# A hybrid streaming-encoder layer on one core: the decay chain begun directly behind the token factor

## The chip, the cores and the metric

The kernel runs on one core of a Trainium2 chip. The metric is the device time of one execution in microseconds (us). Five engines work beside each other and meet only through semaphores: TensorE (PE in the profile, its weight loads PEld), VectorE (DVE), ScalarE (ACT), GpSimd (POOL) and SyncE (SP), whose queue issues most of the transfers.

## The reference

One layer of a trunk over 512 tokens with 1024 channels, all in float32. What matters here is the first part:

```python
xn = rmsnorm(h, mix_norm_w)
proj = xn @ w_in                      # gates, gMLP, z, xBC, dt
...
xbc = jax.nn.silu(causal_dwconv(xbc, conv_w, conv_b))      # 4 taps; xs, B, C
dt = jax.nn.softplus(dt_raw + dt_bias)
A = -jnp.exp(a_log)
...
a_cum = jnp.cumsum(dt * A, axis=2)
decay = jnp.exp(where(causal, a_cum[l] - a_cum[s], -inf))
y_diag = einsum(C·B, decay, x * dt);  states and y_off use exp(a_cum)
```

Behind it come a gated gMLP branch, the projections of both branches, a ConvGLU feed-forward part and a last RMSNorm. None of that is touched.

## The kernel before

Channels lie on the 128 partitions and the 512 tokens in the free dimension. Every projection goes through `cols`: a unit of 256 output channels fills two PSUM accumulators of 128x512, from two halves (`kb`) of four input tiles each. To keep float32 precision each operand is split in a high and a low part (ACT copies the high part, DVE subtracts), and each product takes three matmuls, so a unit of K=1024 is 48 matmuls of 128x512. The weights come through `weights`, with four buffers each for the raw, high and low parts.

The normalisation is postponed. The first two units (`B0` and `C0`, a half of B and of C) multiply the input times the norm's weight (`xw`), not yet divided by the token's root mean square. Meanwhile the token factor `rb` is made (`x_norm`: sums by matmuls, a power on POOL, a broadcast by matmuls, a copy on ACT). Then `unnorm` scales the finished accumulators by `rb`, and `x_split` makes the normalised, split input `xn` for all later units.

The order of the work from there on is: `C0`, then the units `x0`, `x2`, `x4`, `x6` (xs, channels 0 to 1023), `B2`, `C2`, then `x8` to `x14`. Each unit is followed by `conv`, on both accumulators: ACT starts the sum from PSUM (L341), DVE adds three shifted taps from PSUM (L343), ACT applies Silu (L345). An accumulator comes free at the third tap. There are four such PSUM buffers in rotation (`PM`), so a unit waits until the convolution of the unit two before has read its accumulators: `x8p` needs those of `B2p`, `x10p` those of `C2p`.

The decay chain `dt_chain` is a generator in pieces: dt_raw scaled by `rb` (`dtraw`), its transposes (`dttok`), the softplus as a row of some twenty small DVE instructions (`dttmp`, 128x128), the cumulative sums as two matmuls (`acp`), copies and exponentials of these (`ac_k`, `decb`, `dd_k`), transposes (`ach`), and two copies (`achs`, `eahs`) that go out to DRAM (`acum_d`, `ea_d`). Each `ssm_step` loads them back, broadcast over the partitions (`s0bc`, `s0ea` for the first pair of heads), and the decay matrices are made from these.

`defer` and `tick` say in which step of the matmul loop a piece is recorded: each `kb` of `cols` is one tick. The table `CHAIN` holds the ticks for the pieces of the chain. That is the order of recording. In it, PE is written out by hand for the first two units only (`manual_schedule`); from there a scheduler with a model of the engines sets the order on PE, ACT, DVE, POOL and the SP queue. Engines take their instructions strictly in that order.

Of the kernel before, what the change touches and what calls it, by code (L numbers as in the profile page):

```python
# [33 lines left out]
def kernel(  # L34
# [15 lines left out]
    def T(name, dt=F32):  # L50
        return tp.tile([P, S], dt, tag="t", name=name)
# [4 lines left out]
    def PA(name):  # L56
        return pp.tile([P, S], F32, tag="aux", name=name, bufs=4)
# [31 lines left out]
    def cols(w, u, xs, name):  # L89

        K = len(xs)
        ps = [PM(f"{name}p{i}") for i in range(2)]
        nb = K // 4
        for kb in range(nb):
            hi, lo = weights(w[u, kb], [P, 4, 2 * P], f"{name}w{kb}")

            def mm(i, k, part):
                xh, xl = xs[4 * kb + k]
                c = slice(i * P, (i + 1) * P)
                if part == 0:  # L100
                    pe.matmul(ps[i], lhsT=hi[:, k, c], rhs=xh, start=(kb == 0 and k == 0), stop=False)  # L101
                    pe.matmul(ps[i], lhsT=hi[:, k, c], rhs=xl, start=False, stop=False)  # L102
                else:
                    pe.matmul(ps[i], lhsT=lo[:, k, c], rhs=xh, start=False, stop=(kb == nb - 1 and k == 3))  # L104

            if name in BYK:
                order = [(i, k, part) for k in range(4) for part in range(2) for i in range(2)]
            elif kb < nb - 1:
                order = [(i, k, part) for part in range(2) for k in range(4) for i in range(2)]
            else:  # L110
                order = [(i, k, part) for i in range(2) for part in range(2) for k in range(4)]
            for o in order:
                mm(*o)
            tick()
        return ps
# [4 lines left out]
    def defer(fn, n=1):  # L120
        later.append([n, fn])
# [86 lines left out]
    def rstd(ssq, n, name):  # L208

        m = ssq.shape[-1]  # L210
        v = sm.tile([P, m], F32, tag="rsv", name=name + "v")
        dve.tensor_scalar(out=v, in0=ssq, scalar1=1.0 / n, scalar2=EPS, op0=ALU.mult, op1=ALU.add)  # L212
        r = sm.tile([P, m], F32, tag="rsr", name=name + "r")
        pool.tensor_tensor(out=r, in0=v, in1=mhalf[:, :m], op=ALU.pow)  # L214
        return r

    def token_sums(sq, name):

        ps = PA(name)
        n = sq.shape[-1] // P  # L220
        for c in range(n):
            pe.matmul(ps[:, 2 * c:2 * c + 2], lhsT=sq[:, c * P:(c + 1) * P], rhs=ones[:, 0:2], start=True, stop=True)
        return ps[:, 0:2 * n].rearrange("p (c t) -> p c t", t=2)[:, :, 0]

    def bcast_tokens(r, name):

        ps = PA(name)
        n = r.shape[-1]
        for c in range(n):
            pe.matmul(ps[:, c * P:(c + 1) * P], lhsT=r[:, c:c + 1].to_broadcast([P, P]), rhs=ident,  # L230
                      start=True, stop=True)
        return ps[:, 0:n * P]
# [16 lines left out]
    def x_split():  # L249
        ns = []  # L250
        for k in range(KD):
            n = T(f"xn{k}")
            dve.scalar_tensor_tensor(out=n, in0=xT[k], scalar=x0[:, S + k:S + k + 1], in1=rb, op0=ALU.mult, op1=ALU.mult)
            ns.append(n)
            if k:
                xn.append(split(ns[k - 1], f"xn{k - 1}", pool if k in XPOOL else None))
        xn.append(split(ns[-1], f"xn{KD - 1}"))
# [3 lines left out]
    def dt_product():  # L261
        for k in range(KD):
            for i in range(2):
                pe.matmul(dtp[:2 * HEADS], lhsT=wd2[:, k, :], rhs=xw[k][i], start=(k == 0 and i == 0),
                          stop=(k == KD - 1 and i == 1))
# [8 lines left out]
    def flat(t):  # L274
        return t.rearrange("p c h -> p (c h)")

    def dt_chain():

        H = HEADS
        H2 = 2 * H  # L280
        raw = T("dtraw")
        dve.tensor_tensor(out=raw[:H2], in0=dtp[:H2], in1=rb[:H2], op=ALU.mult)
        ps = PA("dttok")
        for c in range(NT):
            pe.transpose(out=ps[:, c * H2:(c + 1) * H2], in_=raw[:H2, c * P:(c + 1) * P], identity=ident[:H2, :H2])
        ps = ps[:, 0:NT * H2].rearrange("p (c h) -> p c h", h=H2)
        tmp = T("dttmp").rearrange("p (i c h) -> p i c h", i=4, h=H)
        xv, e, q, y = (tmp[:, i] for i in range(4))
        dve.tensor_tensor(out=xv, in0=ps[:, :, 0:H], in1=dtb.unsqueeze(1).to_broadcast([P, NT, H]), op=ALU.add)
        dve.tensor_tensor(out=xv, in0=ps[:, :, H:H2], in1=xv, op=ALU.add)  # L290
        act.activation(out=e, in_=xv, func=AF.Abs)
        act.activation(out=e, in_=e, func=AF.Exp, scale=-1.0)
        act.activation(out=alog, in_=alog, func=AF.Exp)
        yield

        with tc.high_priority():
            dve.tensor_scalar(out=q, in0=e, scalar1=2.0, scalar2=None, op0=ALU.add)
            dve.reciprocal(out=q, in_=q)
            dve.tensor_tensor(out=y, in0=e, in1=q, op=ALU.mult)
            dve.tensor_tensor(out=q, in0=y, in1=y, op=ALU.mult)  # L300
            dve.tensor_scalar(out=e, in0=q, scalar1=1.0 / 15, scalar2=None, op0=ALU.mult)
            for d in (13, 11, 9, 7, 5, 3):
                dve.scalar_tensor_tensor(out=e, in0=e, scalar=1.0 / d, in1=q, op0=ALU.add, op1=ALU.mult)
            dve.scalar_tensor_tensor(out=e, in0=e, scalar=1.0, in1=y, op0=ALU.add, op1=ALU.mult)
            dve.tensor_scalar(out=xv, in0=xv, scalar1=0.0, scalar2=None, op0=ALU.max)
            dve.scalar_tensor_tensor(out=dt_k, in0=e, scalar=2.0, in1=xv, op0=ALU.mult, op1=ALU.add)
            dve.scalar_tensor_tensor(out=y, in0=dt_k, scalar=-1.0, in1=alog.unsqueeze(1).to_broadcast([P, NT, H]),
                                     op0=ALU.mult, op1=ALU.mult)

        yield  # L310
        ps = PA("acp")
        pe.matmul(ps[:, 0:P], lhsT=tri, rhs=flat(y), start=True, stop=True)
        pe.matmul(ps[:, P:2 * P], lhsT=ones, rhs=flat(y), start=True, stop=True)
        yield
        act.copy(out=flat(ac_k), in_=ps[:, 0:P])
        act.activation(out=flat(decb), in_=ps[:, P:2 * P], func=AF.Exp)
        dve.tensor_tensor(out=flat(dd_k), in0=ps[:, P:2 * P], in1=flat(ac_k), op=ALU.subtract)
        act.activation(out=dd_k, in_=dd_k, func=AF.Exp)
        dve.tensor_tensor(out=dd_k, in0=dd_k, in1=dt_k, op=ALU.mult)
        pt = PA("ach")  # L320
        for c in range(NT):
            pe.transpose(out=pt[:H, c * P:(c + 1) * P], in_=ac_k[:, c, :], identity=ident)
        yield
        ach = T("achs")
        act.copy(out=ach[:H], in_=pt[:H])
        sync.dma_start(out=acum_d, in_=ach[:H])
        eah = T("eahs")
        act.activation(out=eah[:H], in_=pt[:H], func=AF.Exp)
        sync.dma_start(out=ea_d, in_=eah[:H])
        yield  # L330


    def unnorm(ps, name):
        u = T(name)
        dve.tensor_tensor(out=u, in0=ps, in1=rb, op=ALU.mult)
        return u
# [147 lines left out]
    with tc.manual_schedule(engines={mybir.EngineType.PE}):  # L484
        ps = cols(w_in, U_B, xw, "B0")

        def x_norm():
            r1 = rstd(token_sums(xacc, "xss"), D, "xr")
            dt_product()
            act.copy(out=rb, in_=bcast_tokens(r1, "rbp"))  # L490
            us2.extend(unnorm(ps[q], f"B0u{q}") for q in range(2))
            x_split()

        us2 = []
        defer(x_norm)
        psC = cols(w_in, U_C, xw, "C0")
    us = [unnorm(psC[q], f"C0u{q}") for q in range(2)]
    chain = dt_chain()
    next(chain)
    for n in CHAIN:  # L500
        defer(lambda: next(chain), n)
    for i in (0, 2, 4, 6):
        if i >= 4:
            q = i // 2 - 2
# [263 lines left out]

T_BUFS = 73
XPOOL = ()  # L770
CHAIN = (1, 5, 9, 10)
BYK = ("B0", "x0")
WARM = 10

# [51 lines left out]
```

## Time and profile before

| | |
|---|---|
| time, median of 3 runs | 1027.45 us (1027.16 to 1027.64) |
| the profiled execution | 1028.71 us |
| its span, first to last instruction | 1027.0 us |
| mean granted TensorE clock | 0.995 |
| PE busy | 1014.9 us (99%) |
| DVE busy | 616.5 us (60%) |
| ACT busy | 450.2 us (44%) |
| POOL busy | 41.9 us (4%) |

Busy time is the union of an engine's instructions. In rows of the timeline the columns are the start in us, the length in us, the engine, the line of the kernel, the operation, output and inputs, and how many instructions the row merges; in brackets stands the idle time before it, and what ended that. The matmuls and most others are pipelined: the step from one start to the next is shorter than the length of one.

### The profile page before, as it was taken

To read this page: it belongs to the slowest core of one execution; us is meant where nothing else is said; L and a number is where in the kernel's file an instruction comes from. 1 tells how busy PE (TensorE), PEld (TensorE's weight loads), DVE (VectorE), ACT (ScalarE), POOL (GpSimd) and SP (SyncE) were. 2 spreads that over 40 slices of the span, in tenths; PEclk is the share of its full clock that TensorE was granted. 3 is DMA by queue.
4 is the path that set the end of the run, shared out by engine and by line. 5 is a ranking of instruction groups with operands and counts; after the bars stand their busy time and mean duration, and the time that the engine had idled before them with its cause. 6 is when DMAs were issued, how large, how long until landed. Compare 5 with 4: busy or idle time off the path is not lost.

```text
span 1027.0 us, 12488 instructions
## 1 busy us (share of the span) xinstructions
PE 1014.9 (99%) x4856; PEld 840.3 (82%) x4856; DVE 616.5 (60%) x1006; ACT 450.2 (44%) x613; POOL 41.9 (4%) x72
## 2 busy tenths in 40 slices
PE   9999899999999999999999999999999999999997
PEld 7888788888888888888888888888888888888885
DVE  7795987878796554354123445477668677742224
ACT  7465675665564333363322223354444444331122
POOL 1000000220000200000000000000000000000000
PEclk9999899999999999999999999999999999999999
DMA  7323445423333233323322332232223233323302
GB/s 273 110 83 111 151 144 165 143 94 121 114 125 113 72 97 110 113 85 100 102 97 88 103 102 86 100 114 92 91 93 96 91 101 103 97 89 103 99 25 83
DMA packets 36157, 109.85 MB, mean 107 GB/s; under 512 B 4657, under 2 KB 4929, under 8 KB 36097
## 3 DMA queue, kind: packets, MB, share of 16 engines
q1 hardware_dynamic: 35056, 106.68, 31.8%
q0 software_dynamic: 608, 1.58, 0.5%
q8 instruction: 38, 0.62, 0.3%
q10 hardware_dynamic: 432, 0.79, 0.2%
q14 instruction: 23, 0.18, 0.1%
HBM read 106.80 MB, written 2.24 MB: 106 GB/s over the span
## 4 chain that ended last, share of the span: by engine, by line
PE 98%; DMA 1%; issue 0%; DVE 0%; ACT 0%; POOLq 0%; POOL 0%; SPq 0%
PE dn L726 11%; PE vp L526 1%; PE vp L528 1%; PE vp L527 1%; PE pb6p L101 1%; PE pb4p L101 1%; PE pb2p L101 1%; PE pb0p L101 1%; PE pb6p L104 1%; PE pb4p L104 1%; PE pb2p L104 1%; PE pb0p L104 1%; PE pb6p L102 1%; PE pb4p L102 1%; PE pb2p L102 1%; PE pb0p L102 1%
## 5 line engine op out<-in xcount | busy, mean ns | idle before, releaser
L397 ACT ACT_TABLE_LOAD x15 | 19.2, 1283 | 3.1 <-DMA s15bc<-acum_d 1.6
L764 POOL TENSOR_TENSOR fsr<-fs,mhalf 128x1 f32<-128x1 f32 x4 | 2.2, 548 | 354.9 <-DVE fs L762 354.9
L657 ACT ACTIVATE hh<-hT,pcol 128x512 fp32r<-128x512 f32 x8 | 5.8, 722 | 15.0 <-DVE hT L655 15.0
L756 ACT ACTIVATE fj<-htok 128x512 f32<-128x512 f32 x8 | 5.1, 632 | 16.6 <-DVE htok L754 16.6
L345 ACT ACT_TABLE_LOAD x8 | 10.3, 1283 | 3.9 <-DVE B2c L343 3.0
L214 POOL TENSOR_TENSOR hrr<-hrv,mhalf 128x4 f32<-128x4 f32 x1 | 1.0, 1042 | 248.0 <-DVE hrv L212 248.0
L631 DVE TENSOR_TENSOR m<-m,sa 128x512 f32<-128x512 f32 x8 | 5.5, 688 | 8.6 <-ACT sa L630 8.6
L754 DVE TENSOR_TENSOR htok<-dn,htok 128x512 f32<-128x512 f32 x8 | 5.5, 692 | 8.0 <-PE dn L726 7.9
L612 DVE TENSOR_TENSOR yq<-yq,zs 128x512 f32<-128x512 f32 x12 | 8.2, 685 | 1.5 <-ACT zs L611 1.4
L562 PEld LDWEIGHTS sp<-wsT,v 128*128 128x128 f32 x64 | 7.8, 191 | 0.3
L659 DVE SCALAR_TENSOR_TENSOR hl<-hT,pcol,hh 128x512 fp32r<-128x512 f32 x8 | 6.0, 747 | 3.2 <-ACT hh L657 3.2
L562 PE MATMUL sp<-wsT,v 128*128 128x128 f32 x64 | 7.8, 275 | 0.0
L538 DVE BATCH_NORM_STATS2 bst<-v 128x6 f32<-128x128 f32 x32 | 7.1, 280 | 0.3
L534 ACT ACTIVATE v<-vp 128x512 f32<-128x512 f32 x8 | 4.8, 594 | 3.6 <-PE vp L528 3.6
L565 DVE SCALAR_TENSOR_TENSOR sv<-sp,pcol,radd 128x512 f32<-128x512 f32 x8 | 6.0, 746 | 0.0
L343 DVE SCALAR_TENSOR_TENSOR B2c<-B2p,pcol,B2c 128x511 f32<-128x511 f32 (+2 forms) x6 | 4.2, 742 | 2.5 <-ACT B2c L341 2.5
L694 ACT COPY htok<-htp 128x512 f32<-128x512 f32 x8 | 4.7, 588 | 2.3 <-PE htp L692 2.3
L143 PE MATMUL warm<-ones 128*128 128x128 f32 x20 | 4.6, 429 | 1.1 <-POOL ones L138 1.1
L568 DVE TENSOR_TENSOR sv<-sv,gu 128x512 f32<-128x512 f32 x8 | 5.5, 688 | 0.3
L645 DVE TENSOR_TENSOR sb<-sb,m 128x512 f32<-128x512 f32 x8 | 5.5, 689 | 0.1
L343 DVE SCALAR_TENSOR_TENSOR x14c<-x14p,pcol,x14c 128x511 f32<-128x511 f32 (+2 forms) x6 | 4.5, 747 | 1.5 <-ACT x14c L341 1.4
L743 DVE SCALAR_TENSOR_TENSOR htok<-htok,fsr,fnw 128x512 f32<-128x512 f32 x7 | 5.0, 745 | 0.7 <-POOL fsr L764 0.7
(4034 smaller groups left out, 3501.2 us busy)
## 6 DMA issues: line engine op xcount, KB each, us to landing
out_dram<-htok SPq DMA_DIRECT2D x7, 256.0 KB, 2.0
xT<-in_xt_dram SPq DMA_DIRECT2D x4, 256.0 KB, 6.8
yrb<-yr_d POOLq DMA_DIRECT2D x4, 256.0 KB, 3.5
first<-in_w_in_dram SPq DMA_DIRECT2D x3, 256.0 KB, 7.0
xT<-in_xt_dram POOLq DMA_DIRECT2D x2, 256.0 KB, 7.0
C0w0r<-in_w_in_dram SPq DMA_DIRECT2D x1, 512.0 KB, 7.4
C0w1r<-in_w_in_dram SPq DMA_DIRECT2D x1, 512.0 KB, 7.3
x0w0r<-in_w_in_dram SPq DMA_DIRECT2D x1, 512.0 KB, 5.3
```

Of the source, the lines that this page charges most:

```text
L101: pe.matmul(ps[i], lhsT=hi[:, k, c], rhs=xh, start=(kb == 0 and k == 0), stop=False)
L102: pe.matmul(ps[i], lhsT=hi[:, k, c], rhs=xl, start=False, stop=False)
L104: pe.matmul(ps[i], lhsT=lo[:, k, c], rhs=xh, start=False, stop=(kb == nb - 1 and k == 3))
L343: dve.scalar_tensor_tensor(out=c[:, j:], in0=u[:, :S - j], scalar=pc(R_CW + 24 * (3 - j) + t), in1=c[:, j:], op0=ALU.mult, op1=ALU.add)
L345: act.activation(out=c, in_=c, func=AF.Silu)
L397: act.activation(out=bc, in_=bc, func=AF.Exp)
L526: pe.matmul(ps[t], lhsT=xh[:, ts], rhs=hi[:, k, :], start=(kb == 0 and k == 0), stop=False)
L527: pe.matmul(ps[t], lhsT=xl[:, ts], rhs=hi[:, k, :], start=False, stop=False)
L528: pe.matmul(ps[t], lhsT=xh[:, ts], rhs=lo[:, k, :], start=False, stop=(kb == 3 and k == 1))
L562: pe.matmul(sp[:, t * P:(t + 1) * P], lhsT=vn[t][b][:, gg:gg + P], rhs=wsT[b][:, gg:gg + P], start=True, stop=True)
L612: dve.tensor_tensor(out=acc, in0=acc, in1=zs, op=ALU.add)
L726: pe.matmul(po[t][b], lhsT=l[:, ts], rhs=r[:, cs], start=(k == 0 and l is xh and r is hi), stop=(k == NFF - 1 and r is lo))
```

## The change

The chain's object is created and its first piece recorded inside `x_norm`, directly behind the copy of the token factor, ahead of the scaling of `B0` and of `x_split`. The first piece is cut in two: the multiplication `dtraw` alone, then a new `yield`, then the rest. `CHAIN` gets five entries instead of four. Since `x_norm` runs at the first tick of `C0`, and before the chain was created behind the second and last tick of `C0`, the ticks compare so: the transposes are recorded at the end of `C0` as before, now ahead of the scaling of `C0`'s accumulators, the softplus at the same tick, the cumulative sums at the same tick, the copies behind them and the transposes `ach` one tick earlier, and the two copies to DRAM one tick earlier.

```diff
         dve.tensor_tensor(out=raw[:H2], in0=dtp[:H2], in1=rb[:H2], op=ALU.mult)
+        yield
         ps = PA("dttok")
...
             act.copy(out=rb, in_=bcast_tokens(r1, "rbp"))
+            chain = dt_chain()
+            next(chain)
+            for n in CHAIN:
+                defer(lambda: next(chain), n)
             us2.extend(unnorm(ps[q], f"B0u{q}") for q in range(2))
             x_split()
...
     us = [unnorm(psC[q], f"C0u{q}") for q in range(2)]
-    chain = dt_chain()
-    next(chain)
-    for n in CHAIN:
-        defer(lambda: next(chain), n)
...
-CHAIN = (1, 5, 9, 10)
+CHAIN = (1, 2, 6, 9, 10)
```

The scheduler turns this into another order on every engine, from the first `xs` unit to the gMLP's first unit (`vp`); behind that the rows stand as before. Lines behind the new `yield` count one higher, so L343 of before is L344.

First place, DVE behind the token factor (`rb`); `xn_...` are normalised input tiles, `xn0l` the low part of the first. Before:

```order
L335 TENSOR_TENSOR B0u_326<-B0p_215,rb 128x512
L335 TENSOR_TENSOR B0u_328<-B0p_216,rb 128x512
L253 SCALAR_TENSOR_TENSOR xn_330<-x0m,rb 128x512
L253 SCALAR_TENSOR_TENSOR xn_332<-xT_104,x0m,rb 128x512
L70 TENSOR_TENSOR xn0l<-xn_330,xn0h 128x512
```

The same place on DVE in the changed kernel:

```order
L282 TENSOR_TENSOR dtraw<-dtp,rb 64x512
L336 TENSOR_TENSOR B0u_328<-B0p_215,rb 128x512
L336 TENSOR_TENSOR B0u_330<-B0p_216,rb 128x512
L253 SCALAR_TENSOR_TENSOR xn_332<-x0m,rb 128x512
L253 SCALAR_TENSOR_TENSOR xn_334<-xT_104,x0m,rb 128x512
L70 TENSOR_TENSOR xn0l<-xn_332,xn0h 128x512
```

The multiplication `dtraw` moved from behind all the splits to their head. On PE its four transposes (`dttok`) moved with it, from the middle of `x2` to directly ahead of the first matmul of `x0`.

Second place, ACT around the copies that go to DRAM (`achs`, `eahs`). Before:

```order
L315 COPY ac_k<-acp 128x128
L316 ACT_TABLE_LOAD
L316 ACTIVATE decb<-acp 128x128
L85 ACTIVATE x10w0h<-x10w0r 128x1024
L318 ACTIVATE dd_k<-dd_k 128x128
L325 COPY achs<-ach 32x512
L328 ACTIVATE eahs<-ach 32x512
L341 ACTIVATE B2c_840<-B2p_762,pcol 128x512
L341 ACTIVATE B2c_846<-B2p_763,pcol 128x512
```

The same stretch on ACT in the changed kernel, first the part from `ac_k` on (L346 is the convolutions' Silu):

```order
L316 COPY ac_k<-acp 128x128
L317 ACT_TABLE_LOAD
L317 ACTIVATE decb<-acp 128x128
L346 ACT_TABLE_LOAD
L346 ACTIVATE B0c_676<-B0c_676 128x512
L85 ACTIVATE C2w1h<-C2w1r 128x1024
L346 ACTIVATE C0c_682<-C0c_682 128x512
L342 ACTIVATE x6c_766<-x6p_689,pcol 128x512
L319 ACT_TABLE_LOAD
L319 ACTIVATE dd_k<-dd_k 128x128
L346 ACT_TABLE_LOAD
L346 ACTIVATE x6c_760<-x6c_760 128x512
```

and, following on ACT directly, the part with the two copies:

```order
L326 COPY achs<-ach 32x512
L329 ACT_TABLE_LOAD
L329 ACTIVATE eahs<-ach 32x512
L85 ACTIVATE x8w0h<-x8w0r 128x1024
L346 ACT_TABLE_LOAD
L346 ACTIVATE x6c_766<-x6c_766 128x512
L342 ACTIVATE B2c_840<-B2p_772,pcol 128x512
L85 ACTIVATE x8w1h<-x8w1r 128x1024
L342 ACTIVATE B2c_846<-B2p_773,pcol 128x512
L346 ACTIVATE B2c_840<-B2c_840 128x512
```

The copies stood behind the cast of `x10`'s first weights (`x10w0h`); now they stand ahead of `x8`'s (`x8w0h`), and between `ac_k` and the start of `B2`'s convolution there are six loads of an activation table where there was one. On PE the cumulative sums (`acp`) moved from the middle of `C2` into the last half of `x6`, and the transposes (`ach`) from the end of `C2` into `B2`, behind its first 15 matmuls.

Third place, DVE at the convolution of `B2` (`B2c_840` and `B2c_846`, three taps each, that free the buffers for `x8p`). Before:

```order
L343 SCALAR_TENSOR_TENSOR B2c_840<-B2p_762,pcol,B2c_840 128x511
L343 SCALAR_TENSOR_TENSOR B2c_846<-B2p_763,pcol,B2c_846 128x511
L343 SCALAR_TENSOR_TENSOR B2c_840<-B2p_762,pcol,B2c_840 128x510
L343 SCALAR_TENSOR_TENSOR B2c_846<-B2p_763,pcol,B2c_846 128x510
L86 TENSOR_TENSOR x10w1l<-x10w1r,x10w1h 128x1024
L395 TENSOR_SCALAR s0bc_852<-s0bc_852,ac_k 128x128 x3
L343 SCALAR_TENSOR_TENSOR B2c_840<-B2p_762,pcol,B2c_840 128x509
```

In the changed kernel DVE has there:

```order
L86 TENSOR_TENSOR x8w0l<-x8w0r,x8w0h 128x1024
L344 SCALAR_TENSOR_TENSOR B2c_840<-B2p_772,pcol,B2c_840 128x511
L344 SCALAR_TENSOR_TENSOR B2c_840<-B2p_772,pcol,B2c_840 128x510
L344 SCALAR_TENSOR_TENSOR B2c_840<-B2p_772,pcol,B2c_840 128x509
L86 TENSOR_TENSOR x8w1l<-x8w1r,x8w1h 128x1024
L344 SCALAR_TENSOR_TENSOR B2c_846<-B2p_773,pcol,B2c_846 128x511
L396 TENSOR_SCALAR s0bc_852<-s0bc_852,ac_k 128x128 x4
L344 SCALAR_TENSOR_TENSOR B2c_846<-B2p_773,pcol,B2c_846 128x510
L396 TENSOR_SCALAR s0bc_854<-s0bc_854,ac_k 128x128 x4
L344 SCALAR_TENSOR_TENSOR B2c_846<-B2p_773,pcol,B2c_846 128x509
```

The first accumulator's three taps are done ahead of the first work on the loaded decay rows (`s0bc`); the second one's last two taps still stand behind it. On the SP queue the writes of `acum_d` and `ea_d` moved ahead of the load of `x12w0r`, and the loads of `s0bc` directly behind that, ahead of `x12w1r` and `x14w0r`.

## The prediction

> **What bounds the kernel now.** I read the page first, then who waits for whom, then stretches, then the timeline of each engine around the one stretch that stands out. The page:
>
> ```profile
> span 1027.0 us, 12488 instructions
> PE 1014.9 (99%) x4856; PEld 840.3 (82%) x4856; DVE 616.5 (60%) x1006; ACT 450.2 (44%) x613; POOL 41.9 (4%) x72
> ```
>
> PE bounds the kernel, and the change adds and removes no matmul. So it can only change PE's waits. All of PE's waits (us in total, times, longest):
>
> ```profile
> PE x8p L101 <- DVE B2c L343: 3.5, 1, 3.5
> PE warm L143 <- POOL ones L138: 1.1, 1, 1.1
> PE B0p L101 <- ACT B0w0hi L201: 0.7, 1, 0.7
> ```
>
> The last two lie ahead of anything the change touches. The first is the target. Stretches around it (busy us of PE, PEld, DVE, ACT, POOL; granted clock; DMA), and its matmuls:
>
> ```profile
> 100.00:105.00 5.00, 2.60 (x20) 2.19 (x18) 3.89 (x8) 2.99 (x5) 0.00 (x0) 1.00 0.50 163
> 105.00:110.00 5.00, 3.93 (x9) 3.14 (x10) 5.00 (x14) 3.94 (x5) 0.00 (x0) 0.53 0.92 251
> 110.00:115.00 5.00, 5.00 (x19) 4.02 (x18) 5.00 (x15) 4.09 (x5) 0.00 (x0) 0.79 0.55 188
> ...
> 102.00 0.60 PE L384 MATMUL s0xt<-ident,x0c 128*128 128x128 f32 x4
> 106.07 0.76 PE L101 MATMUL x8p<-xn0h,x8w0h 128*128 128x512 f32 x1 [3.47 <-DVE B2c L343]
> 106.63 0.63 PE L102 MATMUL x8p<-xn0l,x8w0h 128*128 128x512 f32 x1
> 112.15 0.39 PE L101 MATMUL x8p<-xn5h,x8w1h 128*128 128x512 f32 x1
> 112.38 0.40 PE L102 MATMUL x8p<-xn5l,x8w1h 128*128 128x512 f32 x1
> ```
>
> PE stands still for 3.47 us, and then the clock is down: 14 matmuls fill 106.07 to 112.15, 6.08 us, where at the later step (112.38 - 112.15 = 0.23, 0.227 over longer stretches) they take 3.18. The stall costs 3.47 + 2.90 = 6.37 us. What made it, engine by engine:
>
> ```profile
> 88.60 0.39 PE L104 MATMUL B2p<-xn7h,B2w1l 128*128 128x512 f32 x1
> ...
> 97.86 0.58 ACT L325 COPY achs<-ach 32x512 f32<-32x512 f32 x1 [2.21 <-PE ach L322]
> 98.34 0.58 ACT L328 ACTIVATE eahs<-ach 32x512 f32<-32x512 f32 x1
> 98.83 1.42 ACT L341 ACTIVATE B2c<-B2p,pcol 128x512 f32<-128x512 f32 x2
> ...
> 98.47 2.45 DMA acum_d<-achs
> 100.94 3.63 DMA s0bc<-acum_d
> ...
> 104.59 0.68 DVE L395 TENSOR_SCALAR s0bc<-s0bc,ac_k 128x128 f32<-128x128 f32 x3 [1.11 <-DMA s0bc<-acum_d]
> 105.19 0.74 DVE L343 SCALAR_TENSOR_TENSOR B2c<-B2p,pcol,B2c 128x509 f32<-128x509 f32 x1
> ```
>
> `B2p` is complete at 89, but ACT starts its convolution at 98.83, because that stands behind `achs`, which waited for the chain. The last tap then stands on DVE behind `s0bc`, which waits for the chain's round trip through DRAM. The tap ends at 105.93, and `x8p` starts at 106.07. Both queues were blocked by the chain being late.
>
> **The change, part by part.** *The head of the chain.* Its rows:
>
> ```profile
> 42.32 0.70 PE L102 MATMUL x0p<-xn6l,x0w1h 128*128 128x512 f32 x2
> 49.09 0.46 PE L285 MATMUL dttok<-ident,dtraw 64*128 64x64 f32 x4
> ...
> 41.56 0.68 DVE L70 TENSOR_TENSOR xn6l<-xn,xn6h 128x512 fp32r<-128x512 f32 x1
> 43.96 0.67 DVE L282 TENSOR_TENSOR dtraw<-dtp,rb 64x512 f32<-64x512 f32 x1
> ```
>
> `dtraw` ahead of the splits moves each of them back by 0.60 to 0.67 us. There is no room for that: `xn6l` is done at 42.24 and its matmul starts at 42.32. But the transposes now stand ahead of `x0` and move PE back by 0.4 to 0.6 too, time that they took inside `x2` before. I charge the difference, 0.1 us, with 0 and 0.3 as ends.
>
> *The softplus and the sums.*
>
> ```profile
> 72.05 0.74 DVE L343 SCALAR_TENSOR_TENSOR C0c<-C0u,pcol,C0c 128x511 f32<-128x511 f32 x1
> 87.28 0.29 DVE L307 SCALAR_TENSOR_TENSOR dttmp<-dt_k,alog 128x128 f32<-128x128 f32 x1
> ...
> 76.14 0.39 PE L101 MATMUL x6p<-xn6h,x6w1h 128*128 128x512 f32 x1
> 92.01 0.38 PE L312 MATMUL acp<-dttmp,tri 128*128 128x128 f32 x2
> ```
>
> The chain's last small product, done at 87.6 before, now stands directly ahead of that first tap of the second `C0c`, at 72.05 before. Ahead of it come some seven more small steps (0.2 to 0.3 each, as the 0.29 here) and one tap more, so it ends by 72 to 74. The sums now stand behind the `x6p` matmul of 76.14. They find their input ready and run at 76.4 instead of 92.01; `ach` runs at 81.8 (`B2` starts at 78.3, plus 15 times 0.227). PE gains nothing and loses nothing by the moves themselves.
>
> *ACT, the new narrow place.*
>
> ```profile
> 92.65 0.27 ACT L315 COPY ac_k<-acp 128x128 f32<-128x128 f32 x1 [3.47 <-PE acp L313]
> 92.94 1.28 ACT L316 ACT_TABLE_LOAD   x1
> 94.23 0.28 ACT L316 ACTIVATE decb<-acp 128x128 f32<-128x128 f32 x1
> 94.40 1.05 ACT L85 ACTIVATE x10w0h<-x10w0r 128x1024 fp32r<-128x1024 f32 x1
> ...
> 95.89 1.22 DVE L86 TENSOR_TENSOR x10w0l<-x10w0r,x10w0h 128x1024 fp32r<-128x1024 f32 x1
> 99.62 2.73 DVE L343 SCALAR_TENSOR_TENSOR B2c<-B2p,pcol,B2c 128x511 f32<-128x511 f32 x4 [2.52 <-ACT B2c L341]
> ```
>
> From `ac_k` at 77.0 to `achs` ACT has four loads (5.2), three 128-wide steps (0.9), three Silus (0.6 each, from the 0.58 of `eahs`), one weight cast (1.0) and one convolution start (0.7): 9.6 us, so `achs` ends at 87.2, 11 us earlier than before, though `ach` was ready at 82.3. Then a load and `eahs` to 89.1, `x8w0h` to 90.1, a load and a Silu to 92.0, the start of the first `B2c` to 92.7, `x8w1h` to 93.7, the second start to 94.4.
>
> *SP and the round trip.* `acum_d` is written by 87.2 + 2.45 = 89.7. The load of `x12w0r` ahead of `s0bc` waits for DVE's `x8w0l`, 90.1 + 1.2 = 91.3. So `s0bc` is issued at about 91.8. Issue to landing, from the DMA table:
>
> ```profile
> s0bc<-acum_d SPq DMA_DIRECT2D x2, 256.0 KB, 3.8
> s2bc<-acum_d SPq DMA_DIRECT2D x2, 256.0 KB, 8.0
> ```
>
> I take 5, near the row of the same load, with something for the weight load in front; the ends are 3.8 and 8.0. It lands at 96.8 (95.6 to 99.8). DVE meanwhile does the first `B2c` (three taps of 0.68, to 94.8), `x8w1l` (96.0) and one tap of the second (96.7). Behind the landing come 2 x 4 small steps (0.23 each, from 0.68 for three; 1.8) and two taps (1.4): 100.0, at worst 103.0. PE, with nothing missing, ends `s0xt` at 102.6 and needs the second accumulator two matmuls later, at 103.05. The wait is gone over the whole range.
>
> *What is late next: `x10p`,* on the convolution of `C2`:
>
> ```profile
> 119.87 0.83 PE L406 MATMUL s0st<-s0xdd,btok 128*128 128x128 f32 x6
> 120.53 0.60 PE L384 MATMUL s1xt<-ident,x0c 128*128 128x128 f32 x4
> ```
>
> ACT starts it 6.1 us behind the landing (two loads, two exponentials, a cast, a Silu, the start), and DVE needs 10.4 more for what stands there (six taps 4.1, a split 1.2, two rounds of four small steps 1.8, five products of 0.65, as the 0.68 of `xn6l`): landing + 16.5 = 113.3, at worst 116.3. PE wants it at 102.6 + 48 x 0.227 + 1.2 for the two rows + 0.45 = 115.15. Slack 1.9 us; at worst a wait of 1.2. The loads of `x12w0r` and `x12w1r`, on SP behind the chain now, land by 100 and are wanted behind `x10p`, after 125: no price.
>
> *Sum:* -3.47 - 2.90 + 0.1 + 0.1 for small slips = -6.2 us. The profiled execution took 1028.71, 1.7 outside its span and 1.26 above the median. I take the difference as equal in both: 1027.45 - 6.2 = 1021.2.
>
> **The rivals.**
> *A part only (0.20).* Either a wait of 1 to 3.4 us stays at `x8p` or `x10p`, if my ACT sum is some us short: 1022.5 to 1025. Or the half clock behind the stall belongs to the profiled execution alone, and only 3.5 us is won: 1024.0. Three runs within 0.48 us speak against executions that differ by 2.9, so most of the 0.20 is the first case.
>
> [...] The trace shows the clock falling after 3.47 us of idleness.
>
> *No change (0.10), in one of two ways.* First (0.04), ACT's table loads cost more than their rows. [...] The rows speak against it: from the end of `ac_k` (92.92) to `decb` (94.23) pass 1.31 us, the load and nothing else.
>
> [...]
>
> Second (0.06), DVE sets the pace from `x8` on, and PE only meets it later:
>
> ```profile
> 120.00:160.00 40.00, 40.00 (x218) 33.10 (x217) 34.57 (x71) 28.39 (x36) 2.41 (x6) 1.00 0.44 136
> ```
>
> DVE has 5.4 us to spare in 40 there, but PE would come 6.4 earlier. If the convolutions keep their times, the waits come at `x12p` to `vp` and sum to most of the gain: 1026.5 to 1028. Against it: by the sum above `C2` is done 1.9 us before PE wants it, and from there DVE has its 5.4 us in 40 to stay ahead.
>
> *Slower (0.08).* `s0bc`, now in flight with `x12w0r`, lands late. At a landing of 103 the wait at `x8p` is 3.2 and the clock's price about makes it the old stall; from 106 on, 14 us after issue, it is over 1030. The slowest row has 8.0.
>
> **How the numbers follow.** The likeliest, the whole stall gone, gets 0.62: 1021.2 (1020.5 to 1022). With the part case the range is 1020.4 to 1025.2, some 0.82. Half a spread of the runs shown is 0.24 us; 0.2% is 2.05 us, about what a measurement can tell from no change. Faster: 0.62 + 0.20 = 0.82; same 0.10; slower 0.08.
>
> **What would show it.** No PE wait at `x8p`, a granted clock of 1.00 from 100 to 115, `acp` near 76.4, `achs` near 87, `s0bc` landing by 97, `x8p` starting near 102.6, and a span near 1020.8. I am wrong if ACT reaches `achs` after 91, if `x10p`, `x12p` or `vp` wait, or if `x0p` waits over 0.5 us for `xn6l`.

## The result, and the profile after

The changed kernel takes 1021.51 us (median of 4 executions, 1021.38 to 1022.97) against 1027.55 for the kernel before (4, 1027.16 to 1028.52): a ratio of 0.9945 with a 95% interval of 0.9932 to 0.9958. The profiled execution took 1021.54. Its page and all of PE's waits:

```profile
span 1019.8 us, 12484 instructions
PE 1010.8 (99%) x4856; PEld 838.1 (82%) x4856; DVE 616.6 (60%) x1006; ACT 452.3 (44%) x615; POOL 41.4 (4%) x72
...
PE warm L143 <- POOL ones L138: 1.1, 1, 1.1
PE B0p L101 <- ACT B0w0hi L201: 1.0, 1, 1.0
```

The wait of 3.5 us at `x8p` is gone and none has taken its place. The same three stretches as before (PE, PEld, DVE, ACT, POOL busy; granted clock; DMA share; GB/s):

```profile
100.00:105.00 5.00, 5.00 (x32) 4.39 (x31) 3.36 (x5) 4.16 (x6) 0.00 (x0) 1.00 0.55 171
105.00:110.00 5.00, 5.00 (x23) 4.13 (x22) 5.00 (x12) 3.08 (x5) 0.00 (x0) 1.00 0.59 200
110.00:115.00 5.00, 5.00 (x29) 4.31 (x28) 4.81 (x10) 3.75 (x5) 0.00 (x0) 1.00 0.01 2
```

PE is busy throughout (5.00 us in each), at a granted clock of 1.00. Now the chain, in the order in which it runs: the softplus's last product, the sums, the transposes, the two copies, the first start of `B2`'s convolution, the issue and the DMA table's time to landing, the first work on the landed rows, the second accumulator's last tap, the first matmul of `x8p`, and the one that wants the second accumulator:

```profile
71.93 0.30 DVE L308 SCALAR_TENSOR_TENSOR dttmp<-dt_k,alog 128x128 f32<-128x128 f32 x1
76.68 0.38 PE L313 MATMUL acp<-dttmp,tri 128*128 128x128 f32 x2
82.13 0.60 PE L323 MATMUL ach<-ident,ac_k 128*32 128x128 f32 x4
86.74 0.56 ACT L326 COPY achs<-ach 32x512 f32<-32x512 f32 x1
88.61 0.59 ACT L329 ACTIVATE eahs<-ach 32x512 f32<-32x512 f32 x1
92.00 0.76 ACT L342 ACTIVATE B2c<-B2p,pcol 128x512 f32<-128x512 f32 x1
91.83 0.91 SPq L373 DMA_DIRECT2D s0bc<-acum_d  x2
s0bc<-acum_d SPq DMA_DIRECT2D x2, 256.0 KB, 4.3
96.81 0.87 DVE L396 TENSOR_SCALAR s0bc<-s0bc,ac_k 128x128 f32<-128x128 f32 x4
99.04 0.74 DVE L344 SCALAR_TENSOR_TENSOR B2c<-B2p,pcol,B2c 128x509 f32<-128x509 f32 x1
102.67 0.48 PE L101 MATMUL x8p<-xn0h,x8w0h 128*128 128x512 f32 x1
103.22 0.39 PE L101 MATMUL x8p<-xn0h,x8w0h 128*128 128x512 f32 x1
```

The sums run 15.3 us earlier than before, `achs` ends 11.1 us earlier (87.30 against 98.44), and the second accumulator comes free at 99.78, 3.4 us ahead of PE. At `x10p`, the place that was to be late next, the last tap of `C2` and the second accumulator's matmul stand 2.75 us apart:

```profile
111.74 0.73 DVE L344 SCALAR_TENSOR_TENSOR C2c<-C2p,pcol,C2c 128x509 f32<-128x509 f32 x1
115.22 0.39 PE L101 MATMUL x10p<-xn0h,x10w0h 128*128 128x512 f32 x1
```

The spans of the two profiled executions differ by 7.2 us, the medians by 6.0. The experiments show why: executions of the kernel before differ among themselves, and the one that was profiled was a dear one. One further execution, of x2, took 2549.59 us; it is a slow one and is in none of the figures below.

### The profile page after: what moved, and what is told of

Read it like the earlier page. It is cut to its first block, busy times and chain, and to the rows that moved or that the text cites. A ratio compares the mean times of both kernels' runs of the same rounds, so it can differ in the third digit from the quotient of the medians.

```text
span 1019.8 us, 12484 instructions
## 1 busy us (share of the span) xinstructions
PE 1010.8 (99%) x4856; PEld 838.1 (82%) x4856; DVE 616.6 (60%) x1006; ACT 452.3 (44%) x615; POOL 41.4 (4%) x72
## 4 chain that ended last, share of the span: by engine, by line
PE 98%; DMA 0%; issue 0%; DVE 0%; ACT 0%; POOLq 0%; POOL 0%; SPq 0%
PE dn L727 11%; PE vp L527 1%; PE vp L529 1%; PE vp L528 1%; PE pb6p L101 1%; PE pb4p L101 1%; PE pb2p L101 1%; PE pb0p L101 1%; PE pb6p L104 1%; PE pb4p L104 1%; PE pb2p L104 1%; PE pb0p L104 1%; PE pb6p L102 1%; PE pb4p L102 1%; PE pb2p L102 1%; PE pb0p L102 1%
## 5 line engine op out<-in xcount | busy, mean ns | idle before, releaser
L344 DVE SCALAR_TENSOR_TENSOR C2c<-C2p,pcol,C2c 128x511 f32<-128x511 f32 (+2 forms) x6 | 4.5, 742 | 1.6 <-ACT C2c L342 1.6
L344 DVE SCALAR_TENSOR_TENSOR x14c<-x14p,pcol,x14c 128x511 f32<-128x511 f32 (+2 forms) x6 | 4.5, 748 | 1.5 <-ACT x14c L342 1.4
```

The lines of the kernel that those rows point to most:

```text
L344: dve.scalar_tensor_tensor(out=c[:, j:], in0=u[:, :S - j], scalar=pc(R_CW + 24 * (3 - j) + t), in1=c[:, j:], op0=ALU.mult, op1=ALU.add)
```

## The experiments

What the runs gave, for the executions of each kernel; the last column counts those with a mean granted clock of 0.997 or less. The kernel before was run beside each group; its row holds 68 executions of all groups, the 12 of x1 among them; the four of the result are not in it, since their clock is not on record.

| kernel | executions | lowest | median | highest | clock 0.997 or less |
|---|---|---|---|---|---|
| before | 68 | 1025.5 | 1027.6 | 1029.6 | 40 |
| changed | 9 | 1021.2 | 1021.5 | 1023.1 | 0 |
| x2, behind the splits | 5 | 1022.5 | 1022.6 | 1022.6 | 0 |
| x3, first piece only | 6 | 1021.3 | 1021.5 | 1023.1 | 0 |
| x4, 28 redundant transposes | 12 | 1025.8 | 1026.3 | 1029.3 | 0 |
| x6, 12 redundant transposes | 11 | 1025.6 | 1027.9 | 1030.0 | 8 |
| x5, stall without the trip | 7 | 1023.7 | 1024.2 | 1025.7 | 0 |
| x7, lands 2 us later | 5 | 1020.9 | 1021.4 | 1021.5 | 0 |
| x8, lands 7 us later | 12 | 1024.0 | 1025.6 | 1028.0 | 8 |
| x10, 12 warming matmuls | 5 | 1021.4 | 1021.4 | 1021.7 | 0 |
| x11, 14 warming matmuls | 5 | 1021.3 | 1021.6 | 1021.7 | 0 |

The record of the clock is coarse. It reads 1.00 in the first 10 us of an execution whose matmuls run at about half speed there, 0.43 us a step instead of 0.23 (x5, below), and 0.945 in one execution of x1 with an ordinary time (1027.86). Where the text says that the clock fell in so many executions, it says so by this record; only one execution of each kernel (two of the kernel before, two of the changed one) has a trace.

### x1: the kernel before, profiled a second time

> The kernel before, unchanged, as a second profile of it. Mine: the same 3.5 us wait of PE at the third-last xs unit's first matmul (x8p) and 14 matmuls at half clock behind it; time within 0.1% of 1027.5. Rival (the half clock belonged to the one profiled execution): the wait is there, but the granted clock from 105 to 115 is 1.00 and the span about 1024.

Its profiled execution took 1025.93 us, with a span of 1024.2. The stretch behind the wait, and the first two matmuls there:

```profile
105.00:110.00 5.00, 3.91 (x17) 3.28 (x18) 5.00 (x13) 3.92 (x5) 0.00 (x0) 1.00 0.94 214
...
106.09 0.47 PE L101 MATMUL x8p<-xn0h,x8w0h 128*128 128x512 f32 x1 [3.25 <-DVE B2c L343]
106.39 0.40 PE L102 MATMUL x8p<-xn0l,x8w0h 128*128 128x512 f32 x1
```

The wait is there (3.25 us), the half clock isn't: the granted clock is 1.00, and the two matmuls are 0.30 us apart where they were 0.56. `x8p` starts at the same time as in the first profile (106.09 and 106.07), and the first work of `s0st` behind the 48 matmuls at 117.08 instead of 119.87: the clock cost that one 2.79 us and this one nothing. So the rival has the trace of this execution right, and mine the other's. In 40 of the 68 executions of the kernel before the mean clock is 0.997 or less; their median is 1028.40, that of the other 28 is 1026.05.

### x4: PE kept busy in the stall

```diff
-        for c in range(NT):
+        for c in list(range(NT)) * (8 if t == 0 else 1):
             pe.transpose(out=ps[:, c * P:(c + 1) * P], in_=xs[:, c * P:(c + 1) * P], identity=ident)
```

> The kernel before, with the four transposes s0xt made 8 times over (28 redundant transposes of 128x128, some 0.09 to 0.11 us each, 2.5 to 3.1 us): PE works through most of the old stall and stands idle 0.4 to 1 us at most. The convolution of B2 that PE waits for is not made earlier. Mine (half clock is the answer to idleness, and costs every execution 2.9 us): x8p starts at 106 as before, but the granted clock from 105 to 115 is 1.00, and the time is 1027.5 - 2.9 = 1024.6. Rival (only the profiled execution pays for the clock): 1027.5, whatever its profile shows. Rival (the slow matmuls behind the stall have another cause than the idleness): clock about 0.5 there all the same, and 1027.5.

The transposes fill the stall to the last half us, and `x8p` starts no earlier:

```profile
102.17 3.66 PE L384 MATMUL s0xt<-ident,x0c 128*128 128x128 f32 x32
106.28 0.47 PE L101 MATMUL x8p<-xn0h,x8w0h 128*128 128x512 f32 x1 [0.46 <-DVE B2c L343]
```

In none of the 12 executions was the mean clock under 0.998. The lowest time is that of the kernel before with its clock up (1025.83 and 1025.48), the median 1026.33. So, by the record, the clock fell in 40 of 68 executions where PE stood idle (3.25 and 3.47 us in the two profiled), and in 0 of 12 where redundant work left 0.46 us of that. Five of the 12 took 1027.0 us or more all the same, and none of these was traced. The median gains 1.3 us, not the 2.9 that I expected, since the clock did not fall in every execution of the kernel before; the ratio, 0.9992 (0.9981 to 1.0003), doesn't tell it from no change.

### x6: about two us of idleness

The same edit with 4 in place of 8.

> The kernel before, with the transposes s0xt made 4 times over (12 redundant ones, 1.1 to 1.3 us), so that PE stands idle about 2 us at x8p, where the kernel before has 3.2 to 3.5 and the kernel with 28 redundant ones 0.5. In 35 executions of the kernel before 21 had a mean clock of 0.997 or less, in 12 with 28 redundant transposes none. [...] Rival (idleness of any length counts in proportion): half clock in about a third of the executions, and a median between 1026 and 1027.7.

```profile
105.00:110.00 5.00, 3.52 (x11) 2.86 (x12) 5.00 (x14) 3.54 (x4) 0.00 (x0) 0.77 0.95 236
110.00:115.00 5.00, 5.00 (x21) 4.02 (x21) 5.00 (x14) 4.94 (x7) 0.00 (x0) 0.89 0.66 229
...
106.48 0.47 PE L101 MATMUL x8p<-xn0h,x8w0h 128*128 128x512 f32 x1 [2.15 <-DVE B2c L343]
...
107.70 0.59 PE L102 MATMUL x8p<-xn2l,x8w0h 128*128 128x512 f32 x1
...
111.08 0.43 PE L102 MATMUL x8p<-xn4l,x8w1h 128*128 128x512 f32 x1
```

My forecast was a mean clock of 0.998 or more in every execution and a median of 1026, an estimate from the 21 of 35. I was wrong, and so was the size that the rival gave. With some 2 us of idleness (2.15 in the profiled execution) the clock fell in 8 of 11 executions. In the profiled one it even fell after the wait was over: the first five matmuls run at full clock (steps of 0.23 us behind the first), then nine at about half (0.43), from 107.8 to 111.2, some 3.3 us. From the first of `x8p` to `s0st` pass 12.60 us (106.48 to 119.08) where 10.99 do in the second profile (106.09 to 117.08): the clock cost 1.6 us. Ratio 1.0003 (0.9993 to 1.0013).

The half speed of the first profile, from 106.07 to about 112.0, lasted longer than the 3.3 us here. What sets its length, and why the clock of the same program falls in one execution and not in the next, no run shows.

### x5: the stall without the round trip

```diff
+    hops = [dp.tile([HEADS, S], F32, name=f"hop{i}") for i in range(1)]
...
-        sync.dma_start(out=acum_d, in_=ach[:H])
+        for dst, src in zip(hops + [acum_d], [ach[:H]] + hops):
+            sync.dma_start(out=dst, in_=src)
```

> The kernel before, with one redundant copy in DRAM ahead of acum_d, so that s0bc lands about 2 us later. The scheduler then puts both last taps of B2 ahead of all work on s0bc on DVE: x8p no longer hangs on the round trip through DRAM, only on ACT, which starts B2's convolution behind achs as before. Mine (two queues were blocked, ACT's for the longer part): B2's taps end at 99.6 + 2.7 + 1.2 + 1.4 = 104.9, so PE still waits some 2.4 us at x8p instead of 3.5; the time is 1 us under the kernel before with its clock up, 1024.5, and half clock is rarer, median 1024.3 to 1026.5. Rival (the round trip alone made the stall): no wait over 0.5 us at x8p, 1021.5 to 1022.5.

```profile
PE x8p L101 <- DVE B2c L345: 1.7, 1, 1.7
...
99.79 0.58 ACT L326 COPY achs<-ach 32x512 f32<-32x512 f32 x1 [2.21 <-PE ach L323]
105.32 1.39 DVE L345 SCALAR_TENSOR_TENSOR B2c<-B2p,pcol,B2c 128x509 f32<-128x509 f32 x2
108.28 0.87 DVE L397 TENSOR_SCALAR s0bc<-s0bc,ac_k 128x128 f32<-128x128 f32 x4 [0.91 <-DMA s0bc<-acum_d]
```

The taps end ahead of the landing now, and 1.7 us of wait remain. Both queues made the stall: of the 3.25 us of the second profile, 1.55 are the round trip's and 1.7 are ACT's, where `B2c` stands behind `achs`, which waits for `ach`. (All of this execution is 1.7 us later than usual from its first microseconds on; more on that below.) The median is 1024.20, ratio 0.9967 (0.9955 to 0.9978), and the clock fell in none of 7. So bringing the load back earlier would not have been enough by itself; the copies on ACT had to be through earlier too.

### x2 and x3: one part of the change alone

x2 has everything of the change but the head place: the chain is created behind `x_split()`, still inside `x_norm`.

> The changed kernel, but the chain is created behind the splits of the normalised input (behind x_split), at the same tick. Everything of the change stays but the head place. Mine (what counts is that the chain is through some 10 us earlier, not that dtraw stands ahead of the scaling and the splits): no PE wait at x8p, clock 1.00 there, 1021.5 (1020.8 to 1022.5). Rival (the place ahead of the splits is what makes it early): a wait of 1 to 3.5 us comes back at x8p with the half clock, 1024 to 1027.5.

The wait at `x8p` is gone as in the changed kernel, but the time is 1022.58 (ratio 0.9952, 0.9937 to 0.9966), one us more, since there is a new wait. PE and then DVE in x2:

```profile
45.00 0.46 PE L286 MATMUL dttok<-ident,dtraw 64*128 64x64 f32 x4
46.44 0.50 PE L101 MATMUL x2p<-xn0h,x2w0h 128*128 128x512 f32 x1 [0.98 <-DVE C0u L336]
45.49 0.29 DVE L290 TENSOR_TENSOR dttmp<-dttok,dtb 128x128 f32<-128x128 f32 x1 [1.83 <-PE dttok L286]
45.70 1.28 DVE L336 TENSOR_TENSOR C0u<-C0p,rb 128x512 f32<-128x512 f32 x2
```

In x2 `dttok` runs on PE behind `x0`. DVE's first softplus step waits 1.83 us for it, `C0u` waits behind that, and `x2p` needs the accumulators that `C0u` frees. With the chain's head ahead of the splits `dttok` runs at 34.16, `C0u` starts at 43.90, and nobody waits. The head place is worth this 1 us; it isn't what takes the stall away.

x3 is the other part: the first piece stands where the change puts it, but the further pieces keep the old table, counted from the old place.

```diff
+            chain = dt_chain()
+            next(chain)
+            box.append(chain)
             us2.extend(unnorm(ps[q], f"B0u{q}") for q in range(2))
...
-    chain = dt_chain()
+    chain = box[0]
     next(chain)
     for n in CHAIN:
         defer(lambda: next(chain), n)
```

> The kernel before with one part of the change: the chain's first piece (dtraw) is made directly behind the token factor and cut off by the yield, but the other pieces keep their old ticks, so the copies to DRAM are recorded one tick later than in the changed kernel; on ACT x8w0h then stands ahead of achs, and ach on PE behind 23 of B2's matmuls instead of 15. Mine: s0bc lands 1 to 2 us later than in the changed kernel, inside the slack of 3.4 us at x8p: no wait, 1021.5 (1020.8 to 1022.5). Rival (the earlier ticks of the copies are the effective part): a wait of 1 to 3 us at x8p, 1023 to 1027.

1021.54, ratio 0.9944 (0.9930 to 0.9957): all of the gain. The loads were not later, as I had expected, but earlier than in the changed kernel (issued at 91.10 instead of 91.83, first work at 95.42 instead of 96.81): with `x8w0h` ahead of the copies, `x12w0r`, which stands ahead of `s0bc` on SP and waits for `x8w0l`, goes out 2.2 us earlier. So the earlier ticks of the two copies add nothing. Recording `dtraw` inside `x_norm`, cut off from the rest, is enough for the scheduler to carry the whole chain forward.

### x7 and x8: how much slack the changed kernel has

The edit of x5, in the changed kernel, with 2 and with 5 redundant copies.

> The changed kernel, with two redundant copies in DRAM ahead of acum_d and the same order of work on PE, DVE and ACT: s0bc lands some 2 to 4 us later. Mine (the slack at x8p is 103.2 - 99.8 = 3.4 us, at x10p 115.2 - 112.5 = 2.7): if it lands by 99 nothing changes, 1021.5; each us behind 99.5 at x10p is a us of wait. Rival (the changed kernel stands on the edge): a wait of 1 us or more for 2 us, 1022.5 to 1024.

> The changed kernel, with five redundant copies in DRAM ahead of acum_d; the scheduler puts both of B2's last taps ahead of the work on s0bc, but C2's stay behind it. s0bc lands at 103 to 105. Mine (the slack at x10p is all there is left): no wait at x8p, a wait of 0.5 to 2.5 us at x10p, 1022 to 1024, clock up. Rival (DVE makes it good from its idle time): 1021.5. Rival (the wait moves on to x12p, x14p and vp and adds up): 1025 or more.

First work on the landed rows and the last tap of `C2`, in x7 and then in x8, there with the start of `x10p`:

```profile
98.26 0.88 DVE L398 TENSOR_SCALAR s0bc<-s0bc,ac_k 128x128 f32<-128x128 f32 x4 [1.57 <-DMA s0bc<-acum_d]
113.58 0.74 DVE L346 SCALAR_TENSOR_TENSOR C2c<-C2p,pcol,C2c 128x509 f32<-128x509 f32 x1
```

```profile
104.90 0.87 DVE L398 TENSOR_SCALAR s0bc<-s0bc,ac_k 128x128 f32<-128x128 f32 x4 [5.50 <-DMA s0bc<-acum_d]
116.85 0.74 DVE L346 SCALAR_TENSOR_TENSOR C2c<-C2p,pcol,C2c 128x509 f32<-128x509 f32 x1
117.64 0.50 PE L101 MATMUL x10p<-xn0h,x10w0h 128*128 128x512 f32 x1 [2.47 <-DVE C2c L346]
```

In x7 the first work on the rows starts 1.45 us later than in the changed kernel (98.26 against 96.81), and nothing is lost: 1021.37, ratio 0.9936 (0.9925 to 0.9948). In x8 it starts 8.1 us later, but the last tap of `C2` ends only 5.1 us later (117.59 against 112.47): `x10w0l` and `B2`'s last two taps are done ahead of the landing there, and a wait of 1.57 us that DVE had for ACT ahead of `C2`'s first tap is gone. So DVE does make some 3 us good, and my rule that each us behind 99.5 is a us of wait was too strict. Of the 5.1 the slack of 2.75 takes its part, and PE waits 2.47 us at `x10p`. The wait doesn't add up further on, since x8 stands 2.80 us behind x7 at `x12p` (131.15 and 128.35) and 2.81 at `u0p`. The four executions with the clock up took 1024.0 to 1024.4; in 8 of 12 it fell (2.5 us of idleness), and the median is 1025.64 (0.9979, 0.9969 to 0.9990), above what I expected, for the clock again.

### x9 to x11: the first microseconds

x9 is the changed kernel again, x10 and x11 have 12 and 14 in place of 10 for `WARM`.

> The changed kernel, unchanged, as a second profile and as the base for the two kernels beside it. Mine: most executions at 1021.2 to 1021.6, and some 1 in 5 about 1.5 us above, where the clock is still half in the first 10 us; median 1021.5, and 0.9945 of the kernel before.

> The changed kernel with 12 instead of 10 redundant matmuls at its start, that end at about 6.1 us instead of 5.7 (the first real matmul starts at 6.4 to 6.7). Mine (the executions 1.5 us above are those in which the short idleness ahead of the first real matmul lets the clock stay down): fewer of these, the rest as the changed kernel, 1021.4. Rival (the start has nothing to do with it): the same share 1.5 us above.

> The changed kernel with 14 redundant matmuls at its start, that end at about 6.5 us, where the first real matmul starts. Mine: no execution 1.5 us above the others, 1021.4, or up to 0.3 more where the redundant ones delay the first real one. Rival: the same share 1.5 us above.

x9: 1021.55, ratio 0.9951 (0.9938 to 0.9963), one of 5 at 1023.07. Of the changed kernel, x2, x3 and x7, together 25 executions, 3 lie 1.5 us above the rest; of x10 and x11 none in 10. With a share of 3 in 25 that would happen by luck in 0.88 to the tenth, 0.28 of cases: not settled. Late executions with the clock up are more frequent in the kernels that have a stall: 11 of 28 of the kernel before lie at 1027.0 to 1027.8, the other 17 at 1025.5 to 1026.1; in x4 it is 5 of 12, in x5 3 of 7. Why is open, and only one of all these was traced, that of x5. Its matmuls right behind the redundant ones of the start:

```profile
7.13 0.63 PE L102 MATMUL B0p<-xw0l,B0w0hi 128*128 128x512 f32 x1
7.55 0.63 PE L101 MATMUL B0p<-xw0h,B0w0hi 128*128 128x512 f32 x1
...
10.44 0.40 PE L102 MATMUL B0p<-xw1l,B0w0hi 128*128 128x512 f32 x1
```

Up to 10.1 the matmuls run at 0.43 us a step, where the last of these rows has 0.23 behind it (10.67 - 10.44), and `C0p` starts at 19.29 instead of 17.61 (second profile of before). The granted clock of the page's views says 1.00 there; only the step shows it.

## Why the prediction was right

**The sum came out (-6.2 forecast, -6.0 measured), but two of its terms were off, and that one made good most of the other was luck.** The gain, between executions with the clock up (the second profile of before, 1024.2, and after, 1019.8), from the same places of both traces:

```profile
117.75 0.60 PE L384 MATMUL s1xt<-ident,x0c 128*128 128x128 f32 x4
118.28 0.65 PE L422 MATMUL s0y<-s0bc,s0xdt 128*64 128x128 f32 x6
...
129.98 0.87 PE L422 MATMUL s0y<-s0bc,s0xdt 128*64 128x128 f32 x10
130.78 0.71 PE L427 MATMUL s0o<-C0c,s0H 128*128 128x128 f32 x4
...
220.27 0.49 PE L101 MATMUL u0p<-xn0h,u0w0h 128*128 128x512 f32 x1
```

```profile
114.32 0.60 PE L385 MATMUL s1xt<-ident,x0c 128*128 128x128 f32 x4
114.67 0.48 PE L101 MATMUL x10p<-xn0h,x10w0h 128*128 128x512 f32 x1
...
125.74 1.09 PE L423 MATMUL s0y<-s0bc,s0xdt 128*64 128x128 f32 x16
126.77 0.94 PE L428 MATMUL s0o<-C0c,s0H 128*128 128x128 f32 x6
...
215.88 0.49 PE L101 MATMUL u0p<-xn0h,u0w0h 128*128 128x512 f32 x1
```

- *The stall, -3.47: right.* `x8p` starts 3.42 us earlier than in the second profile (102.67 against 106.09).
- *The half clock, -2.90: real where it falls, but not in every execution.* This is the step that failed. I set the clock's price of one profiled execution against a median, and took the agreement of three times within 0.48 us as proof that all paid it. The 1.26 us by which the profiled execution lay above that median was part of this price, and I took it as equal in both kernels. Of 68 executions 40 show the lowered clock, at a median 2.35 us above that of the others and a mean 1.85 above; 40/68 of 1.85 is 1.1 us on the mean. The rival that gave the half clock to the profiled execution alone was as wrong, and its 1024.0 wasn't seen.
- *Behind `x8p`, 0 forecast: 0.97 won.* This I had no term for. From `x8p` to `u0p` before takes 114.18 us, after 113.21, and no wait lies in either. The small matmuls go through in fewer pieces. The `s0y` products of the first head pair were 6 ahead of `x10p`, which started at 118.86, and 10 behind it (0.58 + 0.80 us), and are 16 in one piece now (1.03): 0.35 us less. The four `s1xt`, with `x10p` directly behind them, take 0.35 us instead of 0.53: 0.18 less. Of the rest 0.4 lies in the `vp` stage and was not taken apart; no experiment took this term away by itself, so it is read from the traces and not shown.
- *All three together:* 3.42 + 0.97 + 1.1 = 5.5; the means of the 68 and 9 executions lie 1027.57 - 1021.81 = 5.76 apart. The 0.3 left is about what the late executions with the clock up would give, an estimate: they are 11 of 28 before and 2 of 9 after, and lie some 1.6 us above the rest, so (0.39 - 0.22) x 1.6 = 0.27. Nothing shows that the change has to do with them. Without them and with the clock up the medians are 1025.88 (17 executions) and 1021.48 (7): 4.40 apart, and 3.42 + 0.97 = 4.39.
- *The head, +0.1: not seen.* Between the start of `x0p` and that of `btp` the shifts cancel: `x0p` comes 0.59 later against the second profile, `btp` 0.07, and the start of the first matmul itself differs by 0.12 between the two executions. Its other end, a wait of `x0p` for `xn6l`, did not come.
- *ACT's walk: right to 0.2 us on the copies.* `achs` ended at 87.30 (87.2), `eahs` at 89.20 (89.1), the first `B2c` started at 92.00 (92.0), the second at 93.61 (93.7).
- *The round trip:* issued at 91.83 (91.8), in flight 4.3 us (5 taken), first work at 96.81 (96.8): the landing was earlier, DVE came to it when its other work was done.
- *Slack:* 3.4 us at `x8p` (3.05) and 2.75 at `x10p` (1.9). x8 shows that this second slack was rightly named as what is late next.

Of the rivals, ACT's table loads that cost more than their rows are out. The rows of after:

```profile
77.33 0.27 ACT L316 COPY ac_k<-acp 128x128 f32<-128x128 f32 x1
77.61 1.28 ACT L317 ACT_TABLE_LOAD   x1
78.90 0.28 ACT L317 ACTIVATE decb<-acp 128x128 f32<-128x128 f32 x1
```

The load takes its 1.28 us with 0.02 around it, and two loads more in the whole kernel (38 and 36) brought PE no wait. That DVE sets the pace from `x8` on is out too: no wait up to `vp`. `s0bc` did not land late.

## What to carry to other kernels

When a producer is late, look for every queue that stands behind it before you price the repair: here half of one stall was a transfer's round trip and half was unrelated work behind a waiting copy on ACT, and making the producer early took both away. PE waits of 2.15 us and more (profiled) went with a lowered clock here in some executions and not in others (8 of 11, 8 of 12 and 40 of 68); price such a wait by the share of many executions, not by the profiled one, and don't take three times that agree for a proof that they all pay. Cut off the first small piece of a long chain and record it as soon as its input is there: a scheduler may then carry all the rest forward.

## What the runs showed of the hardware

- PE's clock after idleness, by the recorded clock of the executions and the wait of the one profiled: 0 of 12 fell with 0.46 us idle (profiled), 0 of 7 with 1.7, 8 of 11 with 2.15, 8 of 12 with 2.47, 40 of 68 with 3.25 to 3.47. From 2.15 us on the share did not grow with the length; why is open.
- In x6 the fall came after the wait: five matmuls ran at full clock first (0.23 us a step), then nine in 3.3 us at about half (0.43).
- A row of 32 transposes on PE (3.66 us, 28 of them redundant) in the place of idleness kept the recorded clock at 0.998 or more in 12 of 12 executions (x4).
- In the first 10 us the granted clock of the profile read 1.00 while the matmuls ran at about half speed, 0.43 us a step instead of 0.23 (x5).
